# A macaron decoder layer on one core: table load, first step, mixer halves and last bank taken in another order

## The chip, the core and the metric

The kernel runs on one core of one Trainium2 chip. The metric is the device time of one execution in microseconds (us); the figure for a kernel is the median of its runs. TensorE is PE in the profile (PEld is its weight load), VectorE is DVE, ScalarE is ACT, GpSimd is POOL and SyncE, which issues most transfers, is SP.

## What is computed

One decoder layer on 256 rows of width 2048: a SwiGLU feed-forward block with weight 1/2, a token mixer (pooling means and a gated linear attention), a second feed-forward block with weight 1/2, and a last RMSNorm. Everything is float32.

```python
def rmsnorm(x, g):
    return x * lax.rsqrt(jnp.mean(x * x, axis=-1, keepdims=True) + EPS) * g

def swiglu(h, w_in, w_out):            # w_in 2048 x 11264, w_out 5632 x 2048
    gu = h @ w_in
    gate, up = gu[..., :D_FF], gu[..., D_FF:]
    return (jax.nn.silu(gate) * up) @ w_out

h = h + 0.5 * swiglu(rmsnorm(h, ffn1_norm), ffn1_w_in, ffn1_w_out)
u = rmsnorm(h, mix_norm) @ w_in_mix
y = concat(pool_mixer(u), gla_mixer(u))
h = h + y @ w_out_mix
h = h + 0.5 * swiglu(rmsnorm(h, ffn2_norm), ffn2_w_in, ffn2_w_out)
out = rmsnorm(h, final_norm)
```

## The kernel before

**Products.** Activations stand transposed, 16 k-tiles of 128 by 256 rows (two row tiles t of 128). A float32 product is three matmuls (`three`, L187-190): high part by high part, high by low, low by high. The weights come from HBM in pieces of 1 MB on SP's queue (`load`, L129); `parts_of` makes the high part by a cast on ScalarE (L154) and the low part by a subtraction on VectorE (L155), in blocks of 128x512 that stand in a ring (names ring_hi, ring_lo). For x and h the same is done by `scaled_split` (ScalarE L324, VectorE L325), which also multiplies by the norm's gain.

**Stages.** The first feed-forward block runs up to 708 us, the mixer's input products and the mixer up to 909, its output product up to 1006, the second feed-forward block to the end. Each feed-forward block walks 11 chunks of 512 hidden columns. `first_product` makes a chunk's gate and up: eight steps of two k-tiles, either plain (S) or with seven products in place of eight (W), into PSUM tiles ps_fi or ps_zi of a `Group`. A group has one tile of two banks for each row tile; n = 0 or 1 is the bank, a step's weight has four blocks (k, n). An S step loops over k, then t, then n (L233-236). Silu, transposes and splits follow, and `second_product` multiplies by w_out, into ps_fo or ps_zo. The last group of the second product holds two steps back: `close` (L248) works them off bank by bank, in FFN2 by row tiles, the last bank (1,1) in two halves of 256 columns.

**Start.** x transposed is loaded two k-tiles at a time (`x_ahead`, L584). Eight bf16 matmuls on zeros (L569-571) run while the first data is on its way. ScalarE's first activation is the split of x. The first step's weights come in four transfers, one for each block.

**Between FFN1 and the mixer.** `finish1` (L648) adds the second product to h, then, for the columns 1024 and up, issues both projections (`project`, L624) of the first eight k-tiles, w_mgr (336 columns) and w_mk (512), and then the transposes of the h columns n=2 and n=3 (`transposed_rows`, L420, TensorE L427).

**End.** `finish2` (L976) adds the second product to h (`to_h`, L980), sums squares on ScalarE (L347-349), and `factor` makes 1/sqrt of the mean from them (VectorE, with a power on GpSimd). For n=0 and 1 the last gain is multiplied ahead on GpSimd; at the end each 128x512 piece is multiplied by its row's factor (n=0, 1 on ScalarE, n=2, 3 on VectorE together with the gain) and stored.

The order of instructions on each engine is set by a scheduler that simulates the kernel at build time; the code's order is its starting point.

Of the kernel before, what the change touches and what calls it, by code (L numbers as in the profile page):

```python
# [28 lines left out]
F32 = mybir.dt.float32  # L29
# [52 lines left out]
def layer(ctx: ExitStack, tc: tile.TileContext, io):  # L82
# [109 lines left out]
    class Group:  # L192


        def __init__(self, psum, tags, kinds, name, hold=0, by="t"):
# [5 lines left out]
            self.acc = [  # L201
                psum[tags[0]].tile([P, 2, CW], F32, tag=tags[0], name=f"ps_{name}_{t}")
                for t in range(NT)
            ]
# [14 lines left out]
        def target(self, t, n):  # L219
            key = f"{t}{n}"  # L220
            start = key not in self.fresh
            self.fresh.add(key)
            return self.acc[t][:, n, :], start, self.bound[key] == self.n

        def s(self, a, block):

            self.n += 1
            if self.n > len(self.kinds) - self.hold:
                self.held.append((a, block))
                if self.n == len(self.kinds):  # L230
                    self.close()
                return
            for k in range(2):  # L233
                for t in range(NT):
                    for n in range(2):
                        self.part(a, block, t, n, k, self.bound[f"{t}{n}"] == self.n - 1 and k == 1)

        def part(self, a, block, t, n, k, stop, c=slice(0, CW)):
# [4 lines left out]
            three(  # L243
                self.acc[t][:, n, c], x, (y[0][:, c], y[1][:, c]), start, stop,
                skip_group_check=c.start > 0,
            )

        def close(self):  # L248
# [3 lines left out]
            for t, n in banks:  # L252
                halves = len(self.held) > 1 and self.by == "t" and (t, n) == banks[-1]
                for c in (slice(0, CW // 2), slice(CW // 2, CW)) if halves else (slice(0, CW),):
                    for i, (a, block) in enumerate(self.held):
                        for k in range(2):
                            self.part(a, block, t, n, k, i == len(self.held) - 1 and k == 1, c)

# [175 lines left out]
    def ffn(psum, spool, act, pair, w_in, w_out, row, name, finish, first=None, behind=None):  # L434
# [20 lines left out]
        def first_product(c):  # L455
# [4 lines left out]
            for i, kind in enumerate(kinds):  # L460
# [4 lines left out]
                else:  # L465
# [43 lines left out]
        def second_product(np_, chunks, h):  # L509
# [74 lines left out]
    def x_ahead(kp):  # L584
        if kp in x_in or kp >= KD // 2:
            return
        raw = x_in[kp] = x_raw[kp // 2][:, 2 * (kp % 2) : 2 * (kp % 2) + 2, :]
        nc.sync.dma_start(
            out=raw,
            in_=io["xT"][kp * 2 * P : (kp + 1) * 2 * P, :].rearrange("(k p) t -> p k t", p=P),  # L590
        )

# [383 lines left out]
    def finish2(np_, grp, h):  # L976

        half = CW // 2

        def to_h(t, i, c, ss):  # L980
            to = chunk_of(h, t, 2 * np_ + i)[:, c]
            nc.vector.scalar_tensor_tensor(
                out=to, in0=grp.acc[t][:, i, c], scalar=0.5, in1=to, op0=ALU.mult, op1=ALU.add,
            )
            square_sum(to, ss, f"h3{t}{np_}{i}{c.start}")

        full = slice(0, CW)
        if np_ == 0:
            for t in range(NT):
                for i in range(2):  # L990
                    to = chunk_of(h, t, i)
                    to_h(t, i, full, ss3[:, t, i : i + 1])
                    nc.gpsimd.tensor_tensor(out=to, in0=to, in1=gf[i], op=ALU.mult)
            return

        def factor(t, halves):

            pre = small.tile([P, 3], F32, tag="pre", name=f"pre{t}")
            v = small.tile([P, 1], F32, tag="fv", name=f"fin_v{t}")
            to_h(t, 0, full, ss3[:, t, 2:3])  # L1000
            if halves:
                to_h(t, 1, slice(0, half), ss3[:, t, 3:4])
                to_h(t, 1, slice(half, CW), pre[:, 1:2])
            else:
                to_h(t, 1, full, ss3[:, t, 3:4])
# [7 lines left out]
            if halves:
                nc.vector.scalar_tensor_tensor(
                    out=v, in0=pre[:, 1:2], scalar=1.0 / D, in1=d, op0=ALU.mult, op1=ALU.add
                )
            r = small.tile([P, 1], F32, tag="fr", name=f"fin_r{t}")
# [8 lines left out]

        r = [factor(t, t == 1) for t in range(NT)]
        for t in range(NT):
            rows = slice(t * P, (t + 1) * P)
            for n in (2, 0, 3, 1):  # L1030
                s = slice(n * CW, (n + 1) * CW)
                to = chunk_of(h, t, n)
                if n < 2:
                    nc.scalar.activation(out=to, in_=to, func=AF.Copy, scale=r[t])
                    nc.scalar.dma_start(out=io["out"][rows, s], in_=to)
                else:
                    nc.vector.scalar_tensor_tensor(
                        out=to, in0=to, scalar=r[t], in1=gf[n], op0=ALU.mult, op1=ALU.mult
                    )
                    nc.sync.dma_start(out=io["out"][rows, s], in_=to)  # L1040

# [90 lines left out]
```

## Time and profile before

| what | value |
|---|---|
| runs | 1715.77, 1715.08, 1714.83 us, median 1715.08 |
| profiled execution | 1714.64 us, of which the profile's span is 1712.9 |
| granted TensorE clock, mean | 0.998 |
| busy TensorE / VectorE / ScalarE / GpSimd | 1699.0 / 1349.0 / 968.5 / 60.7 us |
| transfers | 365.24 MB, mean 213 GB/s |

The span runs from the first to the last instruction that the profiler saw; 1.74 us of the execution lie around it. Rows of the timeline have the start and the duration in us, the engine, the line of the kernel, the operation, out<-in, shapes and the count of instructions put together. In square brackets stands how long the engine was idle before, and what ended that. A matmul's recorded duration is longer than its distance to the next, because they overlap in the pipeline.

### The profile page before, as it was taken

How to read it: one execution, taken by the hardware profiler on the slowest of the kernel's cores; microseconds unless marked ns; L12 is line 12 of the kernel's file. 1: busy time of each engine (PE TensorE's matmuls, PEld its weight loads, DVE VectorE, ACT ScalarE, POOL GpSimd, SP SyncE). 2: the span in 40 equal slices, each digit the busy share in tenths (PEclk: the TensorE clock that was granted, in tenths of full speed). 3: DMA queues.
4: the chain of work that ended last, by engine and by line, in shares of the span. 5: the costliest groups of instructions: out<-in, count | busy, mean ns of one | idle time of the engine just before them, and what ended most of it. 6: DMA issues, size and time to landing. Idle time of an engine off the chain costs nothing.

```text
span 1712.9 us, 20225 instructions
## 1 busy us (share of the span) xinstructions
PE 1699.0 (99%) x7762; PEld 1413.4 (83%) x7762; DVE 1349.0 (79%) x1449; ACT 968.5 (57%) x1228; POOL 60.7 (4%) x69
## 2 busy tenths in 40 slices
PE   9999999999999999999999999999999999999997
PEld 7888888888888888888988888888888888888886
DVE  8788898989988985554564677989988988988873
ACT  7655565555655563563454564656556556556642
POOL 0000000000000000000000000000000000000011
PEclk9999999999999999999999999999999999999999
DMA  9846856756666575544564664666657667568571
GB/s 345 343 126 245 267 152 245 245 170 237 231 204 214 221 249 204 179 173 142 193 212 172 221 230 139 205 237 222 218 212 245 184 223 245 170 231 264 178 285 50
DMA packets 60020, 365.24 MB, mean 213 GB/s; under 512 B 6786, under 2 KB 9986, under 8 KB 21267
## 3 DMA queue, kind: packets, MB, share of 16 engines
q1 hardware_dynamic: 51810, 335.61, 54.3%
q0 software_dynamic: 7392, 27.27, 7.5%
q8 instruction: 61, 1.00, 0.2%
q10 hardware_dynamic: 720, 1.07, 0.2%
q14 instruction: 37, 0.30, 0.0%
HBM read 338.75 MB, written 25.17 MB: 212 GB/s over the span
## 4 chain that ended last, share of the span: by engine, by line
PE 98%; issue 1%; ACT 0%; DVE 0%; DMA 0%; DVEq 0%; POOLq 0%; POOL 0%; ACTq 0%
PE ps_fi L190 19%; PE ps_zi L190 18%; PE ps_fo L190 14%; PE ps_zo L190 13%; PE pw_zi L190 8%; PE pw_fi L190 7%; PE ps_h L190 5%; PE ps_mp L190 3%; PE ps_mv L190 3%; PE ps_mg L190 2%; PE ps_mq L190 1%; PE ps_mk L190 1%; PE ps_mgr L190 1%; PE ztp L498 1%; PE ftp L498 1%
## 5 line engine op out<-in xcount | busy, mean ns | idle before, releaser
L155 DVE TENSOR_TENSOR ring_lo<-ring_raw,ring_hi 128x1024 fp32r<-128x1024 f32 (+6 forms) x427 | 540.6, 1282 | 196.1 <-ACT ring_hi L154 194.9
L154 ACT CAST ring_hi<-ring_raw 128x1024 fp32r<-128x1024 f32 (+2 forms) x515 | 472.0, 942 | 341.0 <-DMA ring_raw<-in_ffn_w_out 44.7
L178 DVE TENSOR_TENSOR ring_raw<-ring_raw 128x512 f32<-128x512 f32 (+1 forms) x195 | 166.3, 864 | 0.9
L190 PE MATMUL ps_fi<-ring_hi,xT_hi 128*128 128x512 f32 x298 | 115.7, 393 | 1.8 <-ACT ring_hi L154 1.8
L190 PE MATMUL ps_zi<-ring_lo,h_hi 128*128 128x512 f32 x300 | 117.0, 390 | 0.0
L190 PE MATMUL ps_fi<-ring_lo,xT_hi 128*128 128x512 f32 x298 | 116.8, 392 | 0.0
L190 PE MATMUL ps_zi<-ring_hi,h_lo 128*128 128x512 f32 x300 | 116.8, 390 | 0.0
L190 PE MATMUL ps_zi<-ring_hi,h_hi 128*128 128x512 f32 x300 | 116.6, 390 | 0.0
L190 PE MATMUL ps_fi<-ring_hi,xT_lo 128*128 128x512 f32 x298 | 116.6, 391 | 0.0
L154 ACT CAST zring_hi<-ring_raw 128x1024 fp32r<-128x1024 f32 (+1 forms) x85 | 75.2, 908 | 54.2 <-DMA ring_raw<-in_ffn_w_out 15.2
L190 PE MATMUL ps_zo<-ring_hi,zhi 128*128 128x512 f32 (+1 forms) x262 | 101.9, 389 | 0.0
L190 PE MATMUL ps_zo<-ring_lo,zhi 128*128 128x512 f32 (+1 forms) x262 | 101.7, 388 | 0.0
L190 PE MATMUL ps_zo<-ring_hi,zlo 128*128 128x512 f32 (+1 forms) x262 | 101.4, 388 | 0.0
L155 DVE TENSOR_TENSOR fring_lo<-ring_raw,fring_hi 128x1024 fp32r<-128x1024 f32 (+2 forms) x66 | 86.8, 1325 | 18.5 <-ACT fring_hi L154 18.4
L154 ACT CAST fring_hi<-ring_raw 128x1024 fp32r<-128x1024 f32 (+1 forms) x86 | 76.7, 915 | 42.9 <-issue 11.1
L155 DVE TENSOR_TENSOR zring_lo<-ring_raw,zring_hi 128x1024 fp32r<-128x1024 f32 (+3 forms) x72 | 86.2, 1212 | 15.8 <-ACT zring_hi L154 15.6
L190 PE MATMUL ps_fo<-ring_hi,flo 128*128 128x512 f32 x248 | 97.2, 393 | 0.0
L190 PE MATMUL ps_fo<-ring_hi,fhi 128*128 128x512 f32 x248 | 97.1, 392 | 0.0
L190 PE MATMUL ps_fo<-ring_lo,fhi 128*128 128x512 f32 x248 | 97.0, 391 | 0.0
L155 DVE TENSOR_TENSOR ring_lo<-fring_raw,ring_hi 128x1024 fp32r<-128x1024 f32 (+3 forms) x66 | 79.4, 1213 | 20.2 <-ACT ring_hi L154 20.1
L154 ACT CAST ring_hi<-fring_raw 128x1024 fp32r<-128x1024 f32 (+1 forms) x76 | 69.1, 931 | 22.4 <-DMA fring_raw<-in_ffn_w_out 6.4
L155 DVE TENSOR_TENSOR ring_lo<-zring_raw,ring_hi 128x1024 fp32r<-128x1024 f32 (+3 forms) x45 | 62.9, 1399 | 10.6 <-ACT ring_hi L154 10.0
(316 smaller groups left out, 3801.5 us busy)
## 6 DMA issues: line engine op xcount, KB each, us to landing
ring_raw<-in_ffn_w_in SPq DMA_DIRECT2D x130, 1024.0 KB, 6.1
ring_raw<-in_ffn_w_out SPq DMA_DIRECT2D x68, 1024.0 KB, 7.3
fring_raw<-in_ffn_w_in SPq DMA_DIRECT2D x22, 1024.0 KB, 6.8
zring_raw<-in_ffn_w_in SPq DMA_DIRECT2D x22, 1024.0 KB, 5.2
ring_raw<-in_w_out_mix SPq DMA_DIRECT2D x16, 1024.0 KB, 4.9
fring_raw<-in_ffn_w_out SPq DMA_DIRECT2D x10, 1024.0 KB, 6.9
zring_raw<-in_ffn_w_out SPq DMA_DIRECT2D x10, 1024.0 KB, 7.9
hd<-half_f POOLq DMA_DIRECT2D x18, 512.0 KB, 7.3
```

What stands on the lines that cost most here:

```text
L154: nc.scalar.copy(out=hi[:, j:k, :], in_=src[:, i + j : i + k, :])
L155: nc.vector.tensor_tensor(out=lo, in0=src[:, i : i + n, :], in1=hi.bitcast(F32), op=ALU.subtract)
L178: nc.vector.tensor_tensor(out=out, in0=x, in1=y, op=ALU.subtract)
L190: nc.tensor.matmul(ps, x, y, start=start and i == 0, stop=stop and i == 2, **kw)
L498: nc.tensor.transpose(tp[:, t, k, :], a_t[t][:, k * P : (k + 1) * P], ident)
```

## The change

1. ScalarE copies eight constants to a scratch tile before anything else (`warm`); its first table load now stands in front of that copy.
2. The first two k-tiles of x come in two transfers of one k-tile. The first step of FFN1 goes through its weight blocks in the order in which they are loaded, (0,0), (0,1), (1,1), (1,0) as (k, n). All S steps now loop over blocks outside and row tiles inside.
3. In `finish1` w_mgr's first half is issued, then the transposes of n=2, then w_mk's first half, then the transposes of n=3.
4. In FFN2's last group bank (1,1) has a PSUM tile of its own and is worked off in full width. The mean of a row is built from the first three sums of squares ahead of time, and the fourth is added last. The gain of piece (1, n=2) is multiplied ahead on GpSimd, and the last products are issued in the order n = 3, 0, 2, 1.

```diff
@@ class Group
+            def tile(i, name):
+                return psum[tags[i]].tile([P, 2, CW], F32, tag=tags[i], name=f"ps_{name}")
+            self.acc = [tile(0, f"{self.name}_{t}") for t in range(NT)]
+            self.bank = {(t, n): self.acc[t][:, n, :] for t in range(NT) for n in range(2)}
+            if apart:
+                self.bank[NT - 1, 1] = tile(1, f"{self.name}_last")[:, 0, :]
...
-        def s(self, a, block):
+        def s(self, a, block, order=((0, 0), (0, 1), (1, 0), (1, 1))):
...
-            for k in range(2):
+            last = dict(((n, k) for k, n in order))
+            for k, n in order:
                 for t in range(NT):
-                    for n in range(2):
-                        self.part(a, block, t, n, k, self.bound[f"{t}{n}"] == self.n - 1 and k == 1)
+                    self.part(a, block, t, n, k, self.bound[f"{t}{n}"] == self.n - 1 and k == last[n])
...
-                halves = len(self.held) > 1 and self.by == "t" and (t, n) == banks[-1]
-                for c in (slice(0, CW // 2), slice(CW // 2, CW)) if halves else (slice(0, CW),):
-                    for i, (a, block) in enumerate(self.held):
...
+                for i, (a, block) in enumerate(self.held):
+                    for k in range(2):
+                        self.part(a, block, t, n, k, i == len(self.held) - 1 and k == 1)
@@ first_product, second_product
-                    grp.s(a_of(kp), b)
+                    grp.s(a_of(kp), b, *([((0, 0), (0, 1), (1, 1), (1, 0))] if early and i == 0 else []))
...
+                apart=bool(h) and np_ == 1 and not first,
@@ ahead of the warm-up matmuls
+    nc.scalar.copy(out=small.tile([P, 8], F32, tag="warm", name="warm"), in_=neg_half)
@@ x_ahead
+        src = io["xT"][kp * 2 * P : (kp + 1) * 2 * P, :].rearrange("(k p) t -> p k t", p=P)
+        for ks in (slice(0, 1), slice(1, 2)) if kp == 0 else (slice(0, 2),):
+            nc.sync.dma_start(out=raw[:, ks, :], in_=src[:, ks, :])
@@ finish1
-        if np_ == 1:
-            for w, cw, wname in (("w_mgr", 336, "mgr"), ("w_mk", CW, "mk")):
-                early.append(project(hact, kd, io[w], cw, wname, part=slice(0, KD // 2)))
...
         for n in range(2 * np_, 2 * np_ + 2):
+            if np_ == 1:
+                w, cw = (("w_mgr", 336), ("w_mk", CW))[n % 2]
+                early.append(project(hact, kd, io[w], cw, w, part=slice(0, KD // 2)))
             transposed_rows(
@@ finish2
+        def gain(t, n):
+            to = chunk_of(h, t, n)
+            nc.gpsimd.tensor_tensor(out=to, in0=to, in1=gf[n], op=ALU.mult)
...
+            to_h(t, 0, ss3[:, t, 2:3])
             nc.vector.tensor_reduce(
+                out=pre[:, :1], in_=ss3[:, t, :3], axis=mybir.AxisListType.X, op=ALU.add
+            )
             nc.vector.tensor_scalar(
+                out=pre[:, 1:], in0=pre[:, :1], scalar1=1.0 / D, scalar2=EPS, op0=ALU.mult, op1=ALU.add
+            )
+            if t == NT - 1:
+                gain(t, 2)
+            to_h(t, 1, ss3[:, t, 3:4])
+            nc.vector.scalar_tensor_tensor(
+                out=v, in0=ss3[:, t, 3:4], scalar=1.0 / D, in1=pre[:, 1:], op0=ALU.mult, op1=ALU.add
+            )
...
-            for n in (2, 0, 3, 1):
+            for n in (3, 0, 2, 1):
...
+                if n == 2 and t == NT - 1:
+                    nc.vector.tensor_scalar_mul(to, to, r[t])
                 else:
...
```

TensorE at the start, in the order of before. ps_fi0_0 and ps_fi0_1 are the tiles of row tiles 0 and 1; xT_hi0 and xT_lo0 hold the first four k-tiles.

```order
L190 MATMUL ps_fi0_0_133<-ring_hi_74,xT_hi0_110 128x512
L190 MATMUL ps_fi0_0_133<-ring_lo_75,xT_hi0_110 128x512
L190 MATMUL ps_fi0_0_133<-ring_hi_74,xT_lo0_114 128x512
L190 MATMUL ps_fi0_0_133<-ring_hi_74,xT_hi0_110 128x512
L190 MATMUL ps_fi0_1_134<-ring_hi_74,xT_hi0_110 128x512
L190 MATMUL ps_fi0_1_134<-ring_lo_75,xT_hi0_110 128x512
L190 MATMUL ps_fi0_1_134<-ring_hi_74,xT_lo0_114 128x512
L190 MATMUL ps_fi0_1_134<-ring_hi_74,xT_hi0_110 128x512
```

And in the changed order:

```order
L190 MATMUL ps_fi0_0_135<-ring_hi_74,xT_hi0_112 128x512
L190 MATMUL ps_fi0_1_136<-ring_hi_74,xT_hi0_112 128x512
L190 MATMUL ps_fi0_0_135<-ring_lo_75,xT_hi0_112 128x512
L190 MATMUL ps_fi0_0_135<-ring_hi_74,xT_lo0_116 128x512
L190 MATMUL ps_fi0_1_136<-ring_lo_75,xT_hi0_112 128x512
L190 MATMUL ps_fi0_1_136<-ring_hi_74,xT_lo0_116 128x512
L190 MATMUL ps_fi0_0_135<-ring_hi_74,xT_hi0_112 128x512
L190 MATMUL ps_fi0_1_136<-ring_hi_74,xT_hi0_112 128x512
```

Each block's high part is now used for both row tiles before the first low part is asked for.

TensorE between FFN1 and the mixer, in the order of before. tp_h12 and tp_h13 are the transposes of the h columns n=2 and n=3 (from fh1), h1_hi2 and h1_lo2 the parts made from those of n=2.

```order
L427 MATMUL tp_h12_0_4891<-ident_81,fh1_4419 128x128 x4
L427 MATMUL tp_h12_1_4900<-ident_81,fh1_4419 128x128 x4
L190 MATMUL ps_mgr_4771<-ring_hi_74,h1_hi2_123 128x336
L190 MATMUL ps_mgr_4771<-ring_lo_75,h1_hi2_123 128x336
L190 MATMUL ps_mk_4830<-ring_hi_74,h1_hi2_123 128x512
L190 MATMUL ps_mk_4830<-ring_lo_75,h1_hi2_123 128x512
L190 MATMUL ps_mgr_4771<-ring_hi_74,h1_lo2_127 128x336
L190 MATMUL ps_mk_4830<-ring_hi_74,h1_lo2_127 128x512
L190 MATMUL ps_mgr_4771<-ring_hi_74,h1_hi2_123 128x336
L190 MATMUL ps_mgr_4771<-ring_lo_75,h1_hi2_123 128x336
L190 MATMUL ps_mk_4830<-ring_hi_74,h1_hi2_123 128x512
L190 MATMUL ps_mk_4830<-ring_lo_75,h1_hi2_123 128x512
```

In the changed order, first where the transposes of n=2 stand, then those of n=3 (ps_w_mgr and ps_w_mk are the tiles that were named ps_mgr and ps_mk):

```order
L190 MATMUL ps_w_mgr_4774<-ring_hi_74,h1_lo1_128 128x336
L427 MATMUL tp_h12_0_4833<-ident_81,fh1_4422 128x128 x4
L427 MATMUL tp_h12_1_4842<-ident_81,fh1_4422 128x128 x4
L190 MATMUL ps_w_mk_4851<-ring_hi_74,h1_hi0_123 128x512
L190 MATMUL ps_w_mk_4851<-ring_lo_75,h1_hi0_123 128x512
```

```order
L190 MATMUL ps_w_mk_4851<-ring_hi_74,h1_lo1_128 128x512
L427 MATMUL tp_h13_0_4912<-ident_81,fh1_4422 128x128 x4
L427 MATMUL tp_h13_1_4921<-ident_81,fh1_4422 128x128 x4
L190 MATMUL ps_w_mgr_4774<-ring_hi_74,h1_hi2_125 128x336
L190 MATMUL ps_w_mgr_4774<-ring_lo_75,h1_hi2_125 128x336
```

Before, the first product with h1_hi2 came right behind its transposes. Now 48 products of w_mk lie between the two, and behind the transposes of n=3 follow 24 products of w_mgr that use h1_hi2 and h1_lo2 before any uses n=3.

VectorE at the end, in the order of before, from the additions of row tile 0 on (ps_zo1_9_0 and ps_zo1_9_1 are the second product's tiles of row tiles 0 and 1, zh1 is the half of h with n=2 and 3):

```order
L982 SCALAR_TENSOR_TENSOR zh1_11101<-ps_zo1_9_0_11304,zh1_11101 128x512 x2
L1006 TENSOR_REDUCE pre0_11430<-ss_h3_6878 128x1
L1010 TENSOR_SCALAR fin_v0_11431<-pre0_11430 128x1
L1019 SCALAR_TENSOR_TENSOR fin_v0_11431<-fin_v0_11431,fin_r0_11440 128x1
L1022 SCALAR_TENSOR_TENSOR fin_r0_11440<-fin_v0_11431,fin_r0_11440 128x1
L1037 SCALAR_TENSOR_TENSOR zh1_11101<-zh1_11101,fin_r0_11440,gf2_11110 128x512
L1037 SCALAR_TENSOR_TENSOR zh1_11101<-zh1_11101,fin_r0_11440,gf3_11113 128x512
L982 SCALAR_TENSOR_TENSOR zh1_11101<-ps_zo1_9_1_11305,zh1_11101 128x512
L982 SCALAR_TENSOR_TENSOR zh1_11101<-ps_zo1_9_1_11305,zh1_11101 128x256 x2
L1006 TENSOR_REDUCE pre1_11444<-ss_h3_6878 128x1
L1010 TENSOR_SCALAR pre1_11444<-pre1_11444 128x1
L1014 SCALAR_TENSOR_TENSOR fin_v1_11445<-pre1_11444 128x1
```

And in the changed order, where ps_zo1_9_last is the tile of bank (1,1):

```order
L983 SCALAR_TENSOR_TENSOR zh1_11104<-ps_zo1_9_0_11307,zh1_11104 128x512 x2
L1004 TENSOR_REDUCE pre0_11422<-ss_h3_6881 128x1
L1007 TENSOR_SCALAR pre0_11422<-pre0_11422 128x1
L1013 SCALAR_TENSOR_TENSOR fin_v0_11423<-ss_h3_6881,pre0_11422 128x1
L983 SCALAR_TENSOR_TENSOR zh1_11104<-ps_zo1_9_1_11308,zh1_11104 128x512
L1018 SCALAR_TENSOR_TENSOR fin_v0_11423<-fin_v0_11423,fin_r0_11433 128x1
L1021 SCALAR_TENSOR_TENSOR fin_r0_11433<-fin_v0_11423,fin_r0_11433 128x1
L1039 SCALAR_TENSOR_TENSOR zh1_11104<-zh1_11104,fin_r0_11433,gf3_11116 128x512
L1039 SCALAR_TENSOR_TENSOR zh1_11104<-zh1_11104,fin_r0_11433,gf2_11113 128x512
L1004 TENSOR_REDUCE pre1_11437<-ss_h3_6881 128x1
L983 SCALAR_TENSOR_TENSOR zh1_11104<-ps_zo1_9_last_11309,zh1_11104 128x512
L1007 TENSOR_SCALAR pre1_11437<-pre1_11437 128x1
```

The addition of bank (1,0) has moved ahead of row tile 0's last products, and one addition of the last bank stands in the place of two of 256 columns.

Elsewhere the engines have the same work. On ScalarE and VectorE some ten places around the ends of chunks have two neighbouring rows swapped (a weight's cast or split against another one, or against the silu or the eviction of the transposes); around the third chunk of FFN1 the first W step's casts and splits are taken in another order.

More of the change, by code (lines that the diff above doesn't have):

```diff
@@ L192, in layer, with __init__ @@
     class Group:
-        def __init__(self, psum, tags, kinds, name, hold=0, by="t"):
+        def __init__(self, psum, tags, kinds, name, hold=0, by="t", apart=False):
             self.psum, self.tags, self.kinds, self.name = psum, tags, kinds, name
@@ L200, in __init__ @@
             self.held = []
[L201 to L204, printed above, removed]
+            def tile(i, name):
[4 more added lines that the diff above has]
+                self.bank[NT - 1, 1] = tile(1, f"{self.name}_last")[:, 0, :]
             self.n = 0
@@ L222, in target @@
             self.fresh.add(key)
-            return self.acc[t][:, n, :], start, self.bound[key] == self.n
-        def s(self, a, block):
+            return self.bank[t, n], start, self.bound[key] == self.n
+        def s(self, a, block, order=((0, 0), (0, 1), (1, 0), (1, 1))):
             self.n += 1
@@ L243, in part @@
             three(
-                self.acc[t][:, n, c], x, (y[0][:, c], y[1][:, c]), start, stop,
-                skip_group_check=c.start > 0,
+                self.bank[t, n], x, y, start, stop,
             )
@@ L976, in finish2, with to_h @@
     def finish2(np_, grp, h):
-        half = CW // 2
-        def to_h(t, i, c, ss):
-            to = chunk_of(h, t, 2 * np_ + i)[:, c]
+        def to_h(t, i, ss):
+            to = chunk_of(h, t, 2 * np_ + i)
             nc.vector.scalar_tensor_tensor(
-                out=to, in0=grp.acc[t][:, i, c], scalar=0.5, in1=to, op0=ALU.mult, op1=ALU.add,
+                out=to, in0=grp.bank[t, i], scalar=0.5, in1=to, op0=ALU.mult, op1=ALU.add,
             )
-            square_sum(to, ss, f"h3{t}{np_}{i}{c.start}")
-        full = slice(0, CW)
+            square_sum(to, ss, f"h3{t}{np_}{i}")
+        def gain(t, n):
+            to = chunk_of(h, t, n)
+            nc.gpsimd.tensor_tensor(out=to, in0=to, in1=gf[n], op=ALU.mult)
         if np_ == 0:
@@ L990, in finish2, with factor @@
                 for i in range(2):
-                    to = chunk_of(h, t, i)
-                    to_h(t, i, full, ss3[:, t, i : i + 1])
-                    nc.gpsimd.tensor_tensor(out=to, in0=to, in1=gf[i], op=ALU.mult)
+                    to_h(t, i, ss3[:, t, i : i + 1])
+                    gain(t, i)
             return
-        def factor(t, halves):
-            pre = small.tile([P, 3], F32, tag="pre", name=f"pre{t}")
+        def factor(t):
+            pre = small.tile([P, 2], F32, tag="pre", name=f"pre{t}")
             v = small.tile([P, 1], F32, tag="fv", name=f"fin_v{t}")
[L1000 to L1005, printed above, removed]
+            to_h(t, 0, ss3[:, t, 2:3])
             nc.vector.tensor_reduce(
-                out=pre[:, :1], in_=ss3[:, t, :], axis=mybir.AxisListType.X, op=ALU.add
+                out=pre[:, :1], in_=ss3[:, t, :3], axis=mybir.AxisListType.X, op=ALU.add
             )
-            d = pre[:, 2:] if halves else v
             nc.vector.tensor_scalar(
-                out=d, in0=pre[:, :1], scalar1=1.0 / D, scalar2=EPS, op0=ALU.mult, op1=ALU.add
+                out=pre[:, 1:], in0=pre[:, :1], scalar1=1.0 / D, scalar2=EPS, op0=ALU.mult, op1=ALU.add
             )
[L1013 to L1016, printed above, removed]
+            if t == NT - 1:
[4 more added lines that the diff above has]
+            )
             r = small.tile([P, 1], F32, tag="fr", name=f"fin_r{t}")
@@ L1025, in factor @@
             return r
-        r = [factor(t, t == 1) for t in range(NT)]
+        r = [factor(t) for t in range(NT)]
         for t in range(NT):
             rows = slice(t * P, (t + 1) * P)
-            for n in (2, 0, 3, 1):
+            for n in (3, 0, 2, 1):
                 s = slice(n * CW, (n + 1) * CW)
@@ L1035, in finish2 @@
                     nc.scalar.dma_start(out=io["out"][rows, s], in_=to)
+                    continue
+                if n == 2 and t == NT - 1:
+                    nc.vector.tensor_scalar_mul(to, to, r[t])
                 else:
@@ L1039, in finish2 @@
                     )
-                    nc.sync.dma_start(out=io["out"][rows, s], in_=to)
+                nc.sync.dma_start(out=io["out"][rows, s], in_=to)
     ffn(
```

8 lines of the change are left out of this document (1 added, 7 removed).

## The prediction

> **What bounds the kernel now.** I read the page first: engine totals, then the chain that ended last.
>
> ```profile
> PE 1699.0 (99%) x7762; PEld 1413.4 (83%) x7762; DVE 1349.0 (79%) x1449; ACT 968.5 (57%) x1228; POOL 60.7 (4%) x69
> PE 98%; issue 1%; ACT 0%; DVE 0%; DMA 0%; DVEq 0%; POOLq 0%; POOL 0%; ACTq 0%
> ```
>
> TensorE is busy for 99% of the span and carries 98% of the chain. The change takes no product away (the last bank's 24 half-width matmuls become 12 full ones), so only two things can be won: time in which TensorE waits, and the stretch after its last matmul. The view of waits on TensorE says where it waits at all, besides the warm-up matmuls:
>
> ```profile
> PE ps_fi L190 <- ACT ring_hi L154: 1.8, 1, 1.8
> PE ps_mgr L190 <- ACT h_hi L324: 0.6, 1, 0.6
> PE ps_mgr L190 <- DVE h_lo L325: 0.2, 1, 0.2
> ```
>
> One wait at the start, two in the middle (us in total, times, longest). With the tail these are the places of the edits, so the sum has three terms. I read each in the timeline.
>
> **Start: table load, split x transfer, first step block by block.** The timeline of the first 20 us (start, duration, engine):
>
> ```profile
> 0.73 0.44 SPq L588 DMA_DIRECT2D x_raw<-in_xT  x1
> 3.86 1.28 ACT L324 ACT_TABLE_LOAD   x1 [3.86 <-DMA x_raw<-in_xT]
> 5.15 0.91 ACT L324 ACTIVATE xT_hi<-x_raw,gains 128x256 fp32r<-128x256 f32 x2
> 5.96 1.12 ACT L154 CAST ring_hi<-ring_raw 128x512 fp32r<-128x512 f32 x2
> 6.62 0.80 PE L190 MATMUL ps_fi<-ring_hi,xT_hi 128*128 128x512 f32 x1 [1.81 <-ACT ring_hi L154]
> ...
> 9.22 0.63 PE L190 MATMUL ps_fi<-ring_lo,xT_hi 128*128 128x512 f32 x1
> ...
> 9.64 0.63 PE L190 MATMUL ps_fi<-ring_hi,xT_lo 128*128 128x512 f32 x1
> ...
> 10.34 0.39 PE L190 MATMUL ps_fi<-ring_lo,xT_hi 128*128 128x512 f32 x1
> ...
> 10.56 0.39 PE L190 MATMUL ps_fi<-ring_hi,xT_lo 128*128 128x512 f32 x1
> ```
>
> The table load begins only when x has landed. Loaded ahead, the activations start at 3.86 instead of 5.15, and the first matmul comes 1.29 earlier, near 5.33. That counts only if nothing later waits for a clock of its own. The next rows say that something does:
>
> ```profile
> 12.26 1.06 ACT L154 CAST ring_hi<-ring_raw 128x1024 fp32r<-128x1024 f32 x1 [0.25 <-DMA ring_raw<-in_ffn_w_in]
> 13.39 1.22 DVE L155 TENSOR_TENSOR ring_lo<-ring_raw,ring_hi 128x1024 fp32r<-128x1024 f32 x1
> 14.84 0.62 ACT L141 CAST s_f<-sf_f 128x512 fp32r<-128x512 f32 x1 [0.72 <-DVE sf_f L384]
> 15.51 2.00 ACT L154 CAST ring_hi<-ring_raw 128x1024 fp32r<-128x1024 f32 x2
> 17.55 2.29 DVE L155 TENSOR_TENSOR ring_lo<-ring_raw,ring_hi 128x2048 fp32r<-128x2048 f32 x1 [1.34 <-ACT ring_hi L154]
> 19.89 0.50 PE L190 MATMUL ps_fi<-ring_lo,xT_hi 128*128 128x512 f32 x1
> ```
>
> Read backwards: the third step's first low-part matmul starts at 19.89, just behind the end of its split (17.55 + 2.29 = 19.84). That split waited for the cast, the cast stood behind the small s_f cast, that waited for VectorE, which was behind the split at 13.39, whose cast at 12.26 had waited for a transfer. So 19.89 hangs on a landing at about 12.2, and none of these rows changes its place on ScalarE or VectorE. TensorE will arrive about 1.3 us earlier at the third step, issue two high-part matmuls, and wait there. I cost the start at **0**: the chain from 12.2 to 19.84 eats the gain. The extra x issue is one more of 0.44 on SP ahead of all weights, so the landing may come up to 0.44 later. If every weight landing follows the shorter first half of x, it could come about as much earlier. Bounds: -0.4 to +0.4. The (k, n) loops of the other S steps need block n=1 later than before, not earlier: 0 as well, covered by a TensorE that waits nowhere in them.
>
> **Middle: mixer halves between transposes.**
>
> ```profile
> 726.80 1.04 PE L427 MATMUL tp_h<-ident,fh 128*128 128x128 f32 x8
> 731.14 0.60 PE L427 MATMUL tp_h<-ident,fh 128*128 128x128 f32 x4
> 731.49 0.40 PE L190 MATMUL ps_mgr<-ring_hi,h_lo 128*128 128x336 f32 x1
> 731.73 0.32 PE L190 MATMUL ps_mgr<-ring_hi,h_hi 128*128 128x336 f32 x1
> 731.88 0.32 PE L190 MATMUL ps_mgr<-ring_lo,h_hi 128*128 128x336 f32 x1
> ```
>
> From one group of transposes to the next (726.80 to 731.14) pass 4.34 us, with 8 transposes, five 336-column and five 512-column matmuls in them (the order of before has them one by one). At the spacings of undisturbed neighbours (four transposes in 0.35; 0.15 from 731.73 to 731.88; 0.22 from 10.34 to 10.56) these need 0.70 + 0.75 + 1.10 = 2.55. So 1.79 is lost, of which the waits above name 0.8 and the rest is the pipeline running dry and refilling. After the change 48 mk matmuls (10.6 us) lie between the transposes of n=2 and their first use, and 24 mgr matmuls (3.6 us) between those of n=3 and theirs. What must fit into the cover:
>
> ```profile
> 727.00 1.05 ACT L154 CAST ring_hi<-ring_raw 128x1024 fp32r<-128x1024 f32 x1 [2.10 <-PE ps_mk L190]
> 727.96 0.83 ACT L324 ACTIVATE h_hi<-tp_h,gains 128x256 fp32r<-128x256 f32 x2
> ```
>
> Here a cast that waits for TensorE to release a block stands ahead of the evictions. The changed ScalarE order keeps one such cast before the first two evictions of n=3: 1.05 + 0.83 fits into 3.6. A switch between tiles costs a little anyway (731.49 to 731.73 is 0.24, not 0.15), so I take **-1.5**, near the full loss since cover is ample for n=2. Bounds: -0.8 (only the named waits go) and -1.8.
>
> **End: own tile for the last bank, no halves, mean's terms, gain on GpSimd.**
>
> ```profile
> 1699.90 0.28 PE L190 MATMUL ps_zo<-ring_hi,zhi 128*128 128x256 f32 x1
> 1701.02 1.41 DVE L1037 SCALAR_TENSOR_TENSOR zh<-zh,fin_r,gf 128x512 f32<-128x512 f32 x2
> 1702.65 0.28 PE L190 MATMUL ps_zo<-ring_hi,zlo 128*128 128x256 f32 x1
> 1702.97 1.35 DVE L982 SCALAR_TENSOR_TENSOR zh<-ps_zo,zh 128x512 f32<-128x512 f32 x3 [0.54 <-PE ps_zo L190]
> 1703.69 0.63 ACT L349 ACTIVATE sq_h<-zh 128x512 f32<-128x512 f32 x1 [1.27 <-DVE zh L982]
> 1705.03 0.19 ACT L349 ACTIVATION_READ_ACCUMULATOR sq_h<-zh 128x1 f32 x1
> 1705.30 0.16 DVE L1014 SCALAR_TENSOR_TENSOR fin_v<-pre 128x1 f32<-128x1 f32 x1
> 1706.58 1.41 DVE L1037 SCALAR_TENSOR_TENSOR zh<-zh,fin_r,gf 128x512 f32<-128x512 f32 x2
> ```
>
> Now all three additions of row tile 1 wait for the whole tile, and three squares follow in a row: 1703.69 to 1705.30 is 1.61. In the change bank (1,0) is added while TensorE works on the last bank, from about 1700.10 to 1700.82; that delays row tile 0's two products by about 0.25, to 1701.27, done at 1702.68. The last bank's 12 matmuls start until 1699.90 + 11 x 0.227 = 1702.40; a full-width result (0.39 + 0.04 behind its start) is there at 1702.83. So the last addition starts near 1702.85, 0.12 earlier, its square 0.72 later at 1703.57, and then only 0.63 + 0.19 + 0.08 = 0.90 pass until fin_v: 1704.47 instead of 1705.30. Everything behind fin_v keeps its length (the last product without gain is shorter, but the stores behind the first one are not). The term: **-0.83**. Bounds: -0.1 (the squares' gain goes to a late last addition) and -1.0.
>
> The gain of (1,2) is new on GpSimd, beside the products of row tile 0:
>
> ```profile
> 1679.98 7.09 POOL L993 TENSOR_TENSOR zh<-zh,gf 128x512 f32<-128x512 f32 x4 [24.93 <-issue]
> 1682.27 2.40 DVE L155 TENSOR_TENSOR ring_lo<-ring_raw,ring_hi 128x2048 fp32r<-128x2048 f32 x1
> ```
>
> One takes 7.09 / 4 = 1.77; begun at about 1701.65, it ends at 1703.4, a microsecond before GpSimd is needed for fin_r: hidden. A VectorE split within that same GpSimd work took 2.40 instead of 2.29, so the neighbour costs some 5%, 0.04 here. The Trainium skill says otherwise (SBUF — State Buffer, Who interferes with whom): when VectorE reads two SBUF inputs it contends with GpSimd's reads, and the first to issue blocks the other for its whole instruction. By that rule the time would be the one of rival 3. The row of 2.40 speaks against a full block.
>
> **Sum.** Against the profiled execution: 1714.64 + 0 - 1.5 - 0.83 = 1712.3. The profiled execution lies 0.44 below the median of the runs, 1715.08; with that offset the forecast is **1712.7**, 0.14% faster. A measurement of this kernel tells about 0.2% (3.4 us) from no change, so the limits are 1711.6 and 1718.5.
>
> **Rivals** (times with the offset).
> 1. The start gain survives, because the landing at 12.2 comes early or another row than I think binds the third step: 1.29, or half of it where the clock rises at the same 10 us whenever work begins, as the earlier matmuls are then at double spacing (0.42 from 9.22 to 9.64). 1711.4 to 1712.1. Against it: 19.84 and 19.89 fit to 0.05. The Trainium skill (TensorE: Matmul & The Clock Gate, Part 1) has a free-running window of about 3.4 us, by which the rise isn't tied to the first matmul: the smaller of the two prices.
> 2. The middle's gain is half given back: kt 14 of n=3 stands behind a cast that waits for TensorE, like the one at 727.00. 0.8 instead of 1.5, with a late last addition 0.3 more: 1713.4 to 1713.8.
> 3. Full block at the end: GpSimd takes the pair at 1701.96, between the two products, until 1703.73; the second product ends at 1704.43 and the last addition starts 1.65 later than planned. 1712.7 + 1.65 = 1714.4.
> 4. Slower: the scheduler also swapped neighbouring splits and evictions at some ten chunk boundaries of the FFNs. There VectorE is nearly full:
>
> ```profile
> 105.00:130.00 25.00, 25.00 (x112) 20.69 (x111) 23.11 (x25) 16.49 (x20) 1.81 (x2) 1.00 0.57 150
> ```
>
> (VectorE 23.11 of 25 us.) Where TensorE's lead over a split is under its 1.22 us, a swap makes it wait that long; six of them give 7.3 and 1720.0. Against it: TensorE's 25.00 in the same row, and no wait of it listed in either FFN past the first step.
> 5. The change doesn't do what it says, waits merely move: 1715.1.
>
> **How the numbers follow.** Forecast 0.50 (own range 1711.7 to 1713.4), rival 1 0.18, rival 2 0.15, rival 3 0.05, rival 4 0.05, rival 5 0.07. Faster by over 0.2% needs rival 1 with its full price and a good middle, or all bounds at once: 0.22. Slower is rival 4: 0.05. Within: 0.73. The range takes rivals 1, 2, 3 and 5 in: 1711.0 to 1715.3.
>
> **What would show it.** Start: first matmul near 5.3, then a wait of about 1 us for a split near 19.8; a third step that begins its low parts near 18.6 would prove rival 1. Middle: no wait for h_hi or h_lo between 715 and 745. End: fin_v of row tile 1 some 1.7 us behind the last matmul's end (2.4 now). Any new line in the view of waits on TensorE beyond these proves me wrong.

## The result and the profile after

| kernel | median us | lowest to highest | runs | ratio to before, 95% |
|---|---|---|---|---|
| before | 1715.23 | 1714.83 to 1715.77 | 6 | |
| after | 1725.88 | 1725.24 to 1726.25 | 6 | 1.0062 [1.0051, 1.0074] |

The change makes the kernel 10.65 us slower. The prediction was 1712.7, with a range up to 1715.3. The page of the changed kernel, engine totals and the chain that ended last:

```profile
PE 1711.2 (99%) x7750; PEld 1413.5 (82%) x7750; DVE 1349.2 (78%) x1449; ACT 967.3 (56%) x1227; POOL 63.4 (4%) x70
PE 99%; DMA 0%; issue 0%; ACT 0%; POOL 0%; SPq 0%; DVE 0%; POOLq 0%; ACTq 0%
```

TensorE has 12 matmuls fewer and is busy 12.2 us longer (1711.2 against 1699.0); the span grew by 11.4, from 1712.9 to 1724.3. The view of waits on TensorE, complete (us in total, times, longest):

```profile
PE ps_fi L190 <- ACT ring_hi L154: 2.1, 1, 2.1
PE idle L574 <- DVE zeros L569: 1.2, 1, 1.2
```

No wait has been added: both waits of the middle are gone, and the one at the start is 0.3 longer. So the added time is neither waiting nor more work. What is left is the distance from one matmul to the next. The same 100 us of both traces, in the view by windows (busy time and count of each engine, then the granted clock), before:

```profile
1100.00:1200.00 100.00, 100.00 (x451) 82.83 (x450) 91.01 (x94) 62.98 (x77) 3.15 (x4) 1.00 0.68 225
```

and after:

```profile
1100.00:1200.00 100.00, 100.00 (x446) 81.90 (x445) 91.61 (x94) 59.85 (x73) 3.49 (x4) 1.00 0.63 206
```

TensorE is full in both, at a granted clock of 1.00 in both, and issues 446 matmuls where it issued 451. A throttle would show in the clock column; it doesn't. The chain of waits in order of time has a stretch of 51 matmuls without a break (start, us, engine, tile, line, count), before:

```profile
200.05 11.56 PE ps_fi L190 x51
```

and after:

```profile
202.72 11.70 PE ps_fi L190 x51
```

11.56 / 51 is 226.7 ns for one, 11.70 / 51 is 229.4. The view by tile shows the same over a whole stage (minimum/median/maximum ns of one, first start to last start), before:

```profile
L190 PE MATMUL ps_zi<-ring_hi,h_hi x300: 388/390/479, 1006.4 to 1646.6; 128*128 128x512 f32 x150
```

and after:

```profile
L190 PE MATMUL ps_zi<-ring_hi,h_hi x300: 387/389/478, 1012.3 to 1658.1; 128*128 128x512 f32 x150
```

The first products of the second feed-forward block take 640.2 us from first to last start before and 645.8 after. The recorded duration of one matmul (390 and 389) is no guide: matmuls overlap, and only the starts tell their rate.

Following the same matmuls through both traces, this is by how much the changed kernel falls behind or catches up in each stage (worked out from the starts):

| stage | us |
|---|---|
| start, to 30 us | +1.25 |
| FFN1 | +5.6 |
| between FFN1 and the mixer | -1.45 |
| mixer and its output product | +0.5 |
| FFN2, up to its last bank | +5.8 |
| end (the last bank's full-width matmuls and what follows them) | -0.3 |
| sum | +11.4 |

**The edits themselves.** The start, in the timeline of after (start, duration, engine):

```profile
1.17 1.28 ACT L571 ACT_TABLE_LOAD   x1 [1.17 <-PEq L1124]
3.13 0.91 ACT L324 ACTIVATE xT_hi<-x_raw,gains 128x256 fp32r<-128x256 f32 x2 [0.47 <-DMA gains<-in_gains]
6.20 1.27 ACT L154 CAST ring_hi<-ring_raw 128x512 fp32r<-128x512 f32 x2 [2.17 <-DMA ring_raw<-in_ffn_w_in]
6.87 1.22 PE L190 MATMUL ps_fi<-ring_hi,xT_hi 128*128 128x512 f32 x2 [2.06 <-ACT ring_hi L154]
...
11.73 0.63 PE L190 MATMUL ps_fi<-ring_hi,xT_lo 128*128 128x512 f32 x1
...
12.95 0.40 PE L190 MATMUL ps_fi<-ring_lo,xT_hi 128*128 128x512 f32 x1
...
13.18 0.40 PE L190 MATMUL ps_fi<-ring_hi,xT_lo 128*128 128x512 f32 x1
```

The table load and the split of x are early, as planned. But the first weight block's cast had waited 2.17 us for its transfer when it began at 6.20, so the first matmul came at 6.87 and not near 5.3. And the matmuls keep their double spacing until about 12.6, where before it ended at about 10.1.

Between FFN1 and the mixer, after:

```profile
722.77 1.03 PE L427 MATMUL tp_h<-ident,fh 128*128 128x128 f32 x8
723.56 0.47 PE L190 MATMUL ps_w_mk<-ring_hi,h_hi 128*128 128x512 f32 x1
...
734.56 1.03 PE L427 MATMUL tp_h<-ident,fh 128*128 128x128 f32 x8
735.35 0.40 PE L190 MATMUL ps_w_mgr<-ring_hi,h_hi 128*128 128x336 f32 x1
```

Both groups of eight transposes are followed by a product after 0.79 us (722.77 to 723.56, 734.56 to 735.35), with no wait.

The end, after:

```profile
1711.80 0.69 DVE L983 SCALAR_TENSOR_TENSOR zh<-ps_zo,zh 128x512 f32<-128x512 f32 x1 [0.42 <-PE ps_zo L190]
...
1712.85 2.45 DVE L1039 SCALAR_TENSOR_TENSOR zh<-zh,fin_r,gf 128x512 f32<-128x512 f32 x2
...
1713.44 1.30 POOL L990 TENSOR_TENSOR zh<-zh,gf 128x512 f32<-128x512 f32 x1 [1.40 <-issue]
...
1714.10 0.39 PE L190 MATMUL ps_zo_last<-ring_hi,zlo 128*128 128x512 f32 x1
...
1715.29 0.67 DVE L983 SCALAR_TENSOR_TENSOR zh<-ps_zo_last,zh 128x512 f32<-128x512 f32 x1
```

VectorE's two products take 2.45 us where they took 1.41 before. GpSimd's new multiplication runs from 1713.44 to 1714.74, in their middle. So the last addition starts at 1715.29, though its matmul's result was there at about 1714.53 (1714.10 + 0.43): 0.76 lost.

### The profile page after: what moved, and what is told of

It reads as the page before. It is cut to its first block, busy times and chain, and to the rows that moved or that the text cites. A ratio compares the mean times of both kernels' runs of the same rounds, so it can differ in the third digit from the quotient of the medians.

```text
span 1724.3 us, 20194 instructions
## 1 busy us (share of the span) xinstructions
PE 1711.2 (99%) x7750; PEld 1413.5 (82%) x7750; DVE 1349.2 (78%) x1449; ACT 967.3 (56%) x1227; POOL 63.4 (4%) x70
## 4 chain that ended last, share of the span: by engine, by line
PE 99%; DMA 0%; issue 0%; ACT 0%; POOL 0%; SPq 0%; DVE 0%; POOLq 0%; ACTq 0%
PE ps_fi L190 19%; PE ps_zi L190 18%; PE ps_fo L190 14%; PE ps_zo L190 14%; PE pw_zi L190 8%; PE pw_fi L190 7%; PE ps_h L190 5%; PE ps_mp L190 3%; PE ps_mv L190 3%; PE ps_mg L190 2%; PE ps_mq L190 1%; PE ps_w_mk L190 1%; PE ps_w_mgr L190 1%; PE ztp L498 1%; PE ftp L498 1%; PE tp_h L427 0%
## 5 line engine op out<-in xcount | busy, mean ns | idle before, releaser
L190 PE MATMUL ps_zo<-ring_hi,zhi 128*128 128x512 f32 x250 | 98.2, 393 | 0.0
L190 PE MATMUL ps_zo<-ring_lo,zhi 128*128 128x512 f32 x250 | 97.8, 391 | 0.0
L190 PE MATMUL ps_zo<-ring_hi,zlo 128*128 128x512 f32 x250 | 97.6, 392 | 0.0
L155 DVE TENSOR_TENSOR ring_lo<-zring_raw,ring_hi 128x1024 fp32r<-128x1024 f32 (+3 forms) x45 | 62.9, 1398 | 10.5 <-ACT ring_hi L154 10.2
```

The lines of the kernel that those rows point to most:

```text
L155: nc.vector.tensor_tensor(out=lo, in0=src[:, i : i + n, :], in1=hi.bitcast(F32), op=ALU.subtract)
L190: nc.tensor.matmul(ps, x, y, start=start and i == 0, stop=stop and i == 2, **kw)
```

## The experiments

**Theory.** The warm copy writes a new tile, `warm`, in the pool `small` (L571). It takes 32 bytes of each partition, twice, because the pool has two buffers. Every pool that is opened later begins 64 bytes further on: the rings fring and zring (in which a feed-forward block keeps further weights) with their high and low parts, the third tile of W-step factors, the mixer's tiles. The ring `ring`, x, h and the other factors lie ahead of it and stay. In the built programs all large tiles of before begin at an address that leaves 160 when divided by 256 (160 modulo 256); after the change the later ones leave 224. **Theory: the place of the streamed weight block relative to the stationary tile changes the rate of the matmuls.** The rivals were that the new loops of the S steps cost it (operands in another sequence), that the swapped rows on ScalarE and VectorE do, or that the length of the pad matters in itself.

Three kernels separate place from work. **e1_pad64** is the kernel before with nothing but 64 bytes more in `small`:

```diff
+    nc.gpsimd.memset(small.tile([P, 8], F32, tag="pad", name="pad"), 0.0)
```

> The kernel before, with one more scratch tile of 32 bytes (two buffers, 64 bytes) in the pool of small tiles, set to zero on GpSimd at the start and never read. Nothing else changes but that every tile behind that pool, fring and zring among them, lies 64 bytes further. Theory A (place): TensorE reads blocks at their new place more slowly, whatever the loops: about 1726, with matmul distances of 229 to 237 ns wherever fring or zring blocks are read. Theory B (loops over blocks outside, row tiles inside, cost the time): 1715.2, the same as before, with distances of 226 to 228 ns.

**e2_after_in_place** is the change with the warm copy written into a tile that `small` has anyway:

```diff
-    nc.scalar.copy(out=small.tile([P, 8], F32, tag="warm", name="warm"), in_=neg_half)
+    nc.scalar.copy(out=small.tile([P, 1], F32, tag="fr", name="warm"), in_=neg_half[:, :1])
```

> The changed kernel, with its warm-up copy going to a one-column tile of a tag that exists already, so that no tile behind the small pool moves. Theory A (place): the two feed-forward blocks go back to their length of before (11.4 us less between them), and what is left is start, middle and end: 1715.2 + 1.2 - 1.4 - 0.3 = 1714.7, within 1713.5 to 1715.5. Theory B (loops): 1725.9 as with the change.

**e4_loops** is the kernel before with the S steps' new loops alone:

```diff
-                for t in range(NT):
-                    for n in range(2):
+                for n in range(2):
+                    for t in range(NT):
```

> The kernel before with the S steps' loops as in the change (blocks outside, row tiles inside) and nothing else; no tile moves. Theory A (place): 1715.2 within 0.6, distances as before. Theory B (loops): about 1726.

| kernel | median us | lowest to highest | runs | ratio to before, 95% |
|---|---|---|---|---|
| e1_pad64 | 1727.98 | 1727.53 to 1728.53 | 4 | 1.0076 [1.0061, 1.0091] |
| e2_after_in_place | 1714.03 | 1713.01 to 1716.56 | 10 | 0.9994 [0.9985, 1.0004] |
| e4_loops | 1715.44 | 1714.56 to 1715.80 | 10 | 1.0001 [0.9991, 1.0010] |

The pad alone makes the old kernel 12.8 us slower (before in that comparison: 1715.15). The change without its pad has no loss; in their traces TensorE, VectorE, ScalarE and GpSimd work through the same instructions in the same order in e2 and in the change, the swapped rows included. The loops cost nothing that can be measured. The same 51 matmuls in the chain of waits of e1_pad64:

```profile
202.70 11.72 PE ps_fi L190 x51
```

and of e2_after_in_place:

```profile
201.81 11.56 PE ps_fi L190 x51
```

The spacing goes with the pad, not with the edits.

**How far, and modulo what.** The same line with 128, 256 and 512 bytes in `small`, that is with 16, 32 and 64 columns (e3_pad128, e7_pad256, e6_pad512); here the first:

```diff
+    nc.gpsimd.memset(small.tile([P, 16], F32, tag="pad", name="pad"), 0.0)
```

> As e1_pad64 with a scratch tile twice as large: the tiles behind the small pool lie 128 bytes further. Theory A in the form that the place counts modulo 128 bytes: 1715.2, as before. Theory A in the form that any move from the place of before costs (a line of 256 bytes or more, or a collision with other tiles): about 1726 or another number above 1718. Theory B: 1715.2.

> As e1_pad64 with 256 bytes. Period of 256 bytes in the distance: 1715.2. Period of 512 bytes: slower than before by 10 us or more, as with 64 and 128 bytes (which cost 12.8 and 14.6).

> As e1_pad64 with 512 bytes. The operands of one row tile lie 512 bytes from those of the other and were equally fast before, so if only the distance modulo a power of two counts, its period is 512 or less: 1715.2. If any move away from the layout of before costs: about 1727 to 1730.

**Place or distance.** In e5_all64 a tile ahead of everything moves all tiles by 64 bytes, streamed and stationary ones alike:

```diff
+    lead = const.tile([P, 16], F32, name="lead")
+    nc.gpsimd.memset(lead, 0.0)
```

> The kernel before with a scratch tile of 64 bytes at the front of the first pool: every large tile (x and h transposed, ring, fring, zring) lies 64 bytes further, so fring and zring lie where e1_pad64 has them, but their distance to all other tiles is that of before. Theory A1 (the place itself is slow, for example since a block crosses another line): about 1727 or more, since now ring blocks too lie 64 bytes further; with all of some 7,000 matmuls at 229 instead of 226.7 ns it is 1731. Theory A2 (it is the distance between the streamed block and the other operand's tile that counts): 1715.2, distances of 226 to 228 ns.

In e9_blocks64 the 64 bytes stand ahead of `ring`, so that all weight blocks move by the same amount and x, h and nearly all other stationary tiles stay:

```diff
+    nc.gpsimd.memset(units.tile([P, 16], F32, name="gap"), 0.0)
```

> The kernel before with a scratch tile of 64 bytes ahead of the weight buffers: ring, fring and zring all lie 64 bytes further, the transposed x and h, the hidden tiles and most of the S factors (the other operand) stay. Theory A2 (distance between the streamed block and the other operand's tile): now ring blocks are slow too, so nearly all of some 7,000 matmuls of 512 columns take 229 instead of 226.7 ns: 1715.2 + 7,000 x 0.0023 = 1731, at least 1726. Theory A3 (distance between the blocks of ring and of fring, which follow one another): it is that of before, so 1715.2.

And e10_warm256 is the change with a warm tile of 128 bytes, with its two buffers 256:

```diff
-    nc.scalar.copy(out=small.tile([P, 8], F32, tag="warm", name="warm"), in_=neg_half)
+    nc.scalar.copy(out=small.tile([P, 32], F32, tag="warm", name="warm")[:, :8], in_=neg_half)
```

> The changed kernel whole, gain on GpSimd included, with a warm-up tile of 128 bytes in place of 32 (the copy still writes eight columns): fring and zring lie 256 bytes further than before, not 64. Theory A2 with a period of 256 bytes: as e2_after_in_place, 1714.0, between 1713 and 1715.5. If a scratch tile itself or any move costs: 1725 or more.

| kernel | median us | lowest to highest | runs | ratio to before, 95% |
|---|---|---|---|---|
| e3_pad128 | 1729.78 | 1729.38 to 1729.90 | 4 | 1.0086 [1.0070, 1.0101] |
| e7_pad256 | 1715.41 | 1714.64 to 1716.04 | 10 | 1.0001 [0.9991, 1.0010] |
| e6_pad512 | 1714.83 | 1714.54 to 1715.87 | 10 | 0.9998 [0.9988, 1.0007] |
| e5_all64 | 1714.95 | 1714.79 to 1715.75 | 10 | 0.9999 [0.9989, 1.0008] |
| e9_blocks64 | 1729.26 | 1728.95 to 1730.06 | 4 | 1.0083 [1.0070, 1.0097] |
| e10_warm256 | 1713.55 | 1713.21 to 1714.53 | 10 | 0.9991 [0.9982, 1.0000] |

64 and 128 bytes cost, 256 and 512 don't; a period of 128 bytes is refuted by e3_pad128. Moving everything costs nothing, moving one of the two operands does: it is the distance, not the place. e9_blocks64 (expected nearer 1731) also tells a further rival apart, that only neighbouring blocks of rings with unlike places disturb one another: there all rings are moved alike, and it is slow all the same. Mean distance from start to start in the S steps' matmuls (ns, worked out from the traces, from 32 us on), apart by where in a run of matmuls from one ring they stand:

| kernel | fring, zring, from the 7th on | ring, from the 7th on | first four behind a switch |
|---|---|---|---|
| before, and e2, e4 to e8, e10 | 226.7 | 226.7 | 226.9 |
| after | 229.3 | 227.2 | 233.1 |
| e1_pad64 | 230.1 | 227.2 | 233.1 |
| e3_pad128 | 232.9 | 227.1 | 231.3 |
| e9_blocks64 | 229.0 | 229.0 | 229.4 |

The table has two effects. A distance of 64 bytes modulo 256 costs 2.3 to 3.4 ns for every matmul, 128 bytes some 6. And where blocks with and without the shift follow each other, the first four matmuls take 231 to 233 ns, also on the ring that wasn't moved and otherwise stays near 227; in e9, where all rings are moved alike, that is gone. The sum of all distances by the tile written, after less e10_warm256 (equal instructions): ps_fi 2.73, ps_zi 2.44, pw_fi 1.57, pw_zi 1.87, ps_fo 1.29, ps_zo 1.45, together 11.35 us; their medians differ by 12.3.

The stage's view by tile in e9_blocks64 (its line is one further down):

```profile
L191 PE MATMUL ps_zi<-ring_hi,h_hi x300: 388/392/481, 1014.6 to 1660.9; 128*128 128x512 f32 x150
```

and in e5_all64:

```profile
L190 PE MATMUL ps_zi<-ring_hi,h_hi x300: 389/389/478, 1006.7 to 1646.9; 128*128 128x512 f32 x150
```

646.3 us with weight blocks moved alone, 640.2 with both operands moved: the latter is the stage's time before.

**What the edits are worth without the shift.** e8_no_gain is e2 without the new multiplication on GpSimd:

```diff
-            if t == NT - 1:
-                gain(t, 2)
...
-                if n == 2 and t == NT - 1:
-                    nc.vector.tensor_scalar_mul(to, to, r[t])
-                else:
-                    nc.vector.scalar_tensor_tensor(
+                nc.vector.scalar_tensor_tensor(
```

> e2_after_in_place without the gain of piece (1, n=2) on GpSimd; VectorE multiplies by it with the row's factor again, as before. Theory block (GpSimd's product holds VectorE's second product of row tile 0 until it ends, so the last addition starts 0.75 late): the time from the start of the last matmul to the end of the span falls from 10.2 to about 9.45, and the median is 0.75 below that of e2_after_in_place, 1713.3. Theory no block (the last addition waits for something else): 10.2 stays, 1714.0.

e11_more_idle is e8 with 13 warm-up matmuls in place of 8:

```diff
-    for _ in range(8):
+    for _ in range(13):
```

> e8_no_gain with 13 warm-up matmuls on zeros in place of 8, so that TensorE is busy until the first weight block is cast. Theory clock (a later rise of TensorE's clock in some executions is what spreads the start): the rise comes by 7 us, the matmuls of the first step are at 0.227, and the median is lower by 0.3 to 1.0 than that of e8_no_gain, 1712.1 to 1712.8. Theory landing (the weights' landing near 12.2 binds the third step whatever the clock): 1713.0, as e8_no_gain.

e12_old_start is e8 with the whole start of before (no warm copy, x not split, the first step's blocks in the old order):

```diff
-                    grp.s(a_of(kp), b, *([((0, 0), (0, 1), (1, 1), (1, 0))] if early and i == 0 else []))
+                    grp.s(a_of(kp), b)
...
-    nc.scalar.copy(out=small.tile([P, 1], F32, tag="fr", name="warm"), in_=neg_half[:, :1])
...
-        for ks in (slice(0, 1), slice(1, 2)) if kp == 0 else (slice(0, 2),):
+        for ks in (slice(0, 2),):
```

> e8_no_gain with the start of before: no warm-up copy, x's first transfer whole, the first step in the old block order. If the start edits are worth nothing, as predicted (landing binds): 1713.0 within 0.5, as e8_no_gain. If they are worth the 1.3 us that the table load takes: 1714.3. If the later weight landing costs: 1712.6.

| kernel | median us | lowest to highest | runs | ratio to before, 95% |
|---|---|---|---|---|
| e8_no_gain | 1713.05 | 1712.07 to 1714.85 | 10 | 0.9988 [0.9979, 0.9998] |
| e11_more_idle | 1713.32 | 1712.43 to 1714.01 | 11 | 0.9990 [0.9981, 0.9998] |
| e12_old_start | 1713.01 | 1712.48 to 1713.50 | 11 | 0.9986 [0.9977, 0.9995] |

The timeline of e8_no_gain at the end:

```profile
1699.32 0.69 DVE L983 SCALAR_TENSOR_TENSOR zh<-ps_zo,zh 128x512 f32<-128x512 f32 x1 [0.42 <-PE ps_zo L190]
...
1700.37 1.41 DVE L1034 SCALAR_TENSOR_TENSOR zh<-zh,fin_r,gf 128x512 f32<-128x512 f32 x2
...
1701.62 0.39 PE L190 MATMUL ps_zo_last<-ring_hi,zlo 128*128 128x512 f32 x1
...
1702.04 0.69 DVE L983 SCALAR_TENSOR_TENSOR zh<-ps_zo_last,zh 128x512 f32<-128x512 f32 x1 [0.19 <-PE ps_zo_last L190]
```

Without GpSimd's work the two products take 1.41, and the last addition starts 0.42 behind the last matmul's start and waits for TensorE, not for VectorE. From that matmul to the end of the span pass 9.4 us (span 1711.0), in the changed kernel 10.2 (1724.3 - 1714.10). The median is 0.98 lower than e2's, but the two intervals against before overlap; what shows the cause is the two traces.

e11_more_idle has the short spacing of the full clock early, and it gains nothing. TensorE's timeline:

```profile
7.78 0.40 PE L190 MATMUL ps_fi<-ring_hi,xT_lo 128*128 128x512 f32 x1
8.02 0.39 PE L190 MATMUL ps_fi<-ring_hi,xT_hi 128*128 128x512 f32 x1
...
19.80 0.50 PE L190 MATMUL ps_fi<-ring_lo,xT_hi 128*128 128x512 f32 x1 [0.73 <-DVE ring_lo L155]
```

From 7.78 on the spacing is 0.24; TensorE gets ahead and then stands 0.73 us at 19.80 for the third step's split, the very place where the prediction had it wait. In the trace of before that step's first low-part matmul began at 19.89, so the lead is given back there: in these two traces it is the weights' landing that sets the third step, not the clock. That the 13 warm-up matmuls brought the clock up is not shown, since e10's trace has short spacing from 7.79 on with 8 of them. Nor does the median alone exclude a gain of some tenths, because e11's profiled run loses some 1.6 us elsewhere (see what is left open). With the start of before, its S steps' new loops kept (e12_old_start), the kernel is as fast as with the new one (1713.01 and 1713.05). e8_no_gain, e11_more_idle and e12_old_start are the versions whose whole interval against before lies below 1, by 1.9 to 2.3 us or 0.11 to 0.13%.

## Why the prediction was wrong, point by point

**The step that failed** is the second sentence on what bounds the kernel: "The change takes no product away [...], so only two things can be won: time in which TensorE waits, and the stretch after its last matmul." It took the distance between two matmuls for a constant, used "the spacings of undisturbed neighbours" as fixed prices, and so its sum had three terms where a fourth, +12, was due: with the shift the distance in the moved rings is 229.3 ns and not 226.7, and the median 12.3 us higher (1725.88 against e10's 1713.55). Nothing in the trace of before could have priced it, since there every large tile stood at the same place modulo 256; but that `warm` is a new tile, and moves all pools behind it, could be read in the diff. It was weighed as an instruction and not as an allocation. The range failed with it: each of its ends was worked out from waits.

**The test it set itself** failed too. It held that a new line in the view of waits would prove it wrong. There is no new line, and the kernel is 10.65 us slower: a stretch in which TensorE is 100% busy can still be slow.

**Start, 0: size right.** e8 and e12 differ by 0.04 in the median. The way was partly another: the first matmul was not bound by the table, but by the first weight block's landing (the cast at 6.20), so no 1.29 was there to be eaten. The stated obstacle is real: e11 stops at it, at 19.80. Rival 1, worth 0.6 to 1.3, does not show in the medians. In the one profile of after the start is 1.25 behind, because the clock rose near 12.6 instead of 10.1. The Trainium skill (TensorE: Matmul & The Clock Gate, Part 1) has this rise tied to a free-running window of about 3.4 us, so that it varies from run to run; 12.6 and 10.1 lie 2.5 apart in two profiles, which fits. The window itself is not seen here, but the stretches of half clock in e2 and e11 (see what is left open) last about as long.

**S steps' loops, 0: right** (e4_loops 1.0001).

**Middle, -1.5: right** (-1.45 from the starts; distances of ps_mk, ps_mgr and tp_h add up to 44.3 us before, 42.8 after). Rival 2 did not occur.

**End, -0.83: too large by some 0.5.** It came out at about -0.3, with 0.25 of it from the earlier start of the last matmul. The step that failed is that GpSimd's multiplication is hidden and costs its neighbour 5%: the mechanism was rival 3, a product held back by GpSimd. In the changed kernel, the view by tile (minimum/median/maximum ns):

```profile
L1039 DVE SCALAR_TENSOR_TENSOR zh<-zh,fin_r,gf x3: 752/752/1775, 1712.9 to 1718.0; 128x512 f32<-128x512 f32 x3
```

One of the three products took 1.77 us instead of 0.75. The witness against this, a split of 128x2048 that took 2.40 instead of 2.29 beside GpSimd's work, was misread. The prediction gave each of GpSimd's four multiplications the mean, 7.09 / 4 = 1.77. They were not alike; the view by tile and one window of the trace before (length, GpSimd's busy time and count):

```profile
L993 POOL TENSOR_TENSOR zh<-zh,gf x4: 1284/1296/3175, 1680.0 to 1685.8; 128x512 f32<-128x512 f32 x4
1682.65:1685.78 3.13, 3.13 (x1) 1.00 0.00 0
```

Three took about 1.3, and the one beside the split 3.17: it began at 1682.65, behind the split (1682.27 to 1684.67), and ended 1.15 after it. So one engine was held there too; it was GpSimd, which had come second. At the end of the changed kernel GpSimd came first (1713.44) and VectorE's second product, begun at 1713.52, was held: it ended 0.55 behind GpSimd's end, where alone it needs 0.75, so a hold for the whole of GpSimd's 1.30 fits to about 0.2. The Trainium skill (SBUF — State Buffer, Who interferes with whom) has it right: with two SBUF inputs VectorE contends with GpSimd's reads, and who issues first blocks the other for its whole instruction. Rival 3's price, 1.65, was too high, mainly because GpSimd alone takes 1.30 and not 1.77: it was 0.76. Without the multiplication the forecast of the end would have been met: in e8 9.4 us pass from the last matmul's start to the end of the span, in before 10.2 (1712.9 - 1702.65).

**Rival 4** had the right sign by luck, and less than half the size (1720.0 is 4.9 above before, the result 10.65): its swapped splits would show as waits, which the trace of after doesn't have, and e2 and e10 have the same swaps and no loss.

Taken without the shift (e10_warm256, 1713.55; e2, 1714.03), the change is 1.1 to 1.7 us faster than before, not the 2.4 predicted; the interval of e10 reaches to 1.0000.

**Left open:** why a distance that isn't a multiple of 256 bytes costs anything, and why more behind a switch; distances other than 64, 128, 256 and 512 bytes were not tried. In e2's profiled run, its slowest, the spacing doubles for 3.5 us near 756 us (granted clock 0.51 from 755.7 to 759.1), behind matmuls that use 17 rows of the array. In e11's profiled run the same happens near 754 (0.50 from 754.1 to 757.4), which costs some 1.6 us; the trace of after has these matmuls without it. What sets it off, and whether it makes the wide spread of these kernels' times, was not tested.

## What to carry to other kernels

Where TensorE is the bound, a new tile, however small, is an edit to every tile that is allocated behind it: compare the addresses of streamed and stationary tiles before and after, and keep their distance a multiple of 256 bytes (tried here with float32 alone). When an engine is busy longer with no more work and no new wait, count starts over a fixed stretch and divide, since busy shares and recorded durations show nothing. Don't take a mean over a merged row for each of its instructions: look at the smallest and the largest. And repeat a surprising loss with the smallest edit that has only its side effect, here a pad, before explaining it by the edit's purpose.

## What the runs showed of the hardware

float32 matmuls of 128x512 follow each other after 226.7 ns when the streamed and the stationary operand lie a multiple of 256 bytes apart in SBUF, after 229 to 230 ns at 64 bytes and 233 at 128, and with 231 to 233 behind a switch between blocks of unlike distance, at a granted clock of 1.00; on this kernel of 7750 matmuls that is 12 to 15 us. The Trainium skill (SBUF — State Buffer, Who interferes with whom) gives TensorE two independent read ports, for the moving operand and the weight load; if so, these runs suggest that the two streams disturb each other all the same by where they lie; how is not shown.

A VectorE product of two SBUF inputs (128x512) took 1.77 us instead of 0.75 when it began 0.08 behind a GpSimd multiplication of two SBUF inputs; a GpSimd multiplication took 3.17 instead of 1.3 when it began 0.38 behind a VectorE split that lasted 2.40.
